# Cached attention of the decoded rows: one row on 128 partitions, or two rows on 64 each

## The chip, the cores and the metric

The kernel runs on one core of a Trainium2 chip. The core has five engines with an instruction stream each: TensorE (PE in the profile; its weight loads are PEld), VectorE (DVE), ScalarE (ACT), GpSimd (POOL) and SyncE (SP, which here only issues transfers); sixteen DMA engines move data between the device memory and the on-chip memory of 128 partitions. Each stream runs in order and waits on semaphores where it needs another engine's or a transfer's result. The metric is the device time in microseconds of one execution, the median of several runs.

## What is computed

One layer of a decoder on 256 prompt tokens and 8 decoded rows (one token each, with its own caches), D = 2048: a mixing group, cross-attention to 256 memory tokens, and a gated feed-forward part. All is float32. The change touches only the cross-attention of the 8 decoded rows, which read their memory's keys and values from caches:

```python
N_MEM, XA_HEADS, XA_DH = 256, 4, 512          # DEC_BATCH = 8

xq = (rmsnorm(x, g_xa) @ w_xa_q).reshape(B, L, XA_HEADS, XA_DH)
s = jnp.einsum('blhd,bmhd->bhlm', xq, mk) * (XA_DH ** -0.5)
p = jax.nn.softmax(s, axis=-1)
o = jnp.einsum('bhlm,bmhd->blhd', p, mv).reshape(B, L, D_MODEL)
x = x + o @ w_xa_o
```

For a decoded row `mk` and `mv` are `cache_mem_k` and `cache_mem_v` of that row: 4 heads of 256 tokens by 512 features, so 32 tiles (head, row) of 512 KB of keys and as many of values. For the prompt rows `mk` and `mv` are products of the memory with `w_k` and `w_v`, worked out in the same stretch of the kernel.

## The kernel before

**Weights.** The 264 columns (256 tokens and 8 rows) stay on chip; the weights stream past. SP loads them in halves of a step, 512 KB each, into five buffers `raw`. ScalarE copies a half to its high part, VectorE subtracts to get the low part (both into `w`, four buffers), and TensorE makes three products of the parts for each block (`mm`). The list of steps is w_in, w_out, 16 tiles of w_q, then for each of 4 heads 4 of w_k and 4 of w_v, 16 of w_o, and the feed-forward part.

**Order.** Everything beside the weights' products is written as generators that `side` starts and that are advanced between steps by a price for each `yield`; a scheduler that simulates the engines then sets the final order of instructions. Each engine executes its stream in that order. Tiles made by `B(...)` come from one rotating pool of 26 buffers. The helpers that record the engine operations all stand on line 60, so groups are told apart by their tiles.

**Cached attention.** `evac_q` writes the queries of the decoded rows, tile by tile, into `qsm` [128, 16, 8]: partition = feature within a tile of 128, then tile, then row. After the fourth tile `onesr` (128x128 ones) is made and two generators start. `dec_k` goes over heads h and rows b: GpSimd loads the keys `kcT[h, b]` and the values `vcT[h, b]`, each into a fresh tile of `B` [128, 4, 256] (partition = feature, then feature tile, then token); ScalarE makes the first product with the row's query into `dw` [128, 256], VectorE adds the three others, ScalarE copies the result to a high part `ds`, GpSimd subtracts for the low part. `dec_v` sums `ds` over the partitions with two matmuls by `onesr` (the sum is then the same in all partitions, in `ax`), takes the maximum (VectorE), the exponential and its sum (ScalarE, into `ssm`), and multiplies the four value tiles with it in place, each with its sum over tokens into one column of `osm` (VectorE). At most two (head, row) units are between the two generators (`NFL`). When the eight rows of a head are done, `osm` is multiplied by 1 / `ssm` and `st["dh"]` is raised; `attend(h)`, the prompt's attention of that head, waits for that before it folds `osm` into the input of w_o.

The same stretch holds the products of w_q's second part, w_k and w_v, the evictions of those (`B<-mm`, `t<-mm`) and GpSimd's stores of keys and values (`o_k`, `o_v`).

Of the kernel before, what the change touches and what calls it, by code (L numbers as in the profile page):

```python
# [10 lines left out]
F32 = mybir.dt.float32  # L11
F32R = mybir.dt.float32r
I32 = mybir.dt.int32
AF = mybir.ActivationFunctionType
OP = mybir.AluOpType
AX = mybir.AxisListType

P = 128
D = 2048
KC = D // P  # L20
T = 256
NS = 8
N = T + NS
RGB = 8
H = 4
# [16 lines left out]
STEP = object()  # L42
# [52 lines left out]
def layer_kernel(ctx: ExitStack, tc, xT, memT, vec, wrg, w_in, w_out, w_q, w_k, w_v, w_o,  # L95
# [3 lines left out]
    act, dve, pe = Engine(nc.scalar, price_act), Engine(nc.vector, price_dve), Engine(nc.tensor, price_pe)  # L99
    pool_e, sp = nc.gpsimd, nc.sync  # L100

    const = ctx.enter_context(tc.tile_pool(name="const", bufs=1))
# [11 lines left out]
    def nm(s):  # L114
        uid[0] += 1
        return f"{s}_{uid[0]}"

    def B(shape, dt=F32):
        return sb.tile(shape, dt, tag="B", bufs=NB, name=nm("B"))
# [15 lines left out]
    class Arr:  # L135


        def __init__(self, nb, w=N, dt=F32):
            self.t, self.nb, self.w, self.dt = {}, nb, w, dt
# [7 lines left out]
        def __call__(self, c):  # L147
            return self.tile(c // 4)[:, c % 4, :]
# [107 lines left out]
    def by2(x):  # L256

        return x.rearrange("p (a b) -> p a b", b=2)

    def turn(x):  # L260

        return x.rearrange("p (b a) -> p a b", b=2)

    def halves(x):

        return x.rearrange("p (b a) -> p b a", b=2)

    def unturn(ps):

        return ps.rearrange("p (a b) -> p b a", b=2)  # L270
# [9 lines left out]
    st = {}  # L280
# [21 lines left out]
    def side(g, prio=0):  # L302
        x = Gen(g, prio)
        gens.append(x)
        gens.sort(key=lambda q: q.prio)
        return x
# [23 lines left out]
    ones = const.tile([P, P], F32, name="ones")  # L330
    dve.memset(ones, 1.0)
    def bank(tag="mm"):
        return psm.tile([P, 512], F32, tag=tag, bufs=4, name=nm(tag))
# [10 lines left out]
    onesr = const.tile([P, P], F32R, name="onesr")  # L344
# [774 lines left out]
    qsm = const.tile([P, KC, NS], F32, name="qsm")  # L1119
    osm = const.tile([P, KC, NS], F32, name="osm")  # L1120
    ssm = const.tile([P, H, NS], F32, name="ssm")

    def evac_q(j):
        def f(ps):
            if j == 0:
                qn["t"] = Arr(KC, T)
            p2, m = unturn(ps[:, :N]), N // 2
            dve.tensor_mul(qn["t"](j)[:, :m], p2[:, 0, :], rstd[:, :m])
            dve.tensor_mul(qn["t"](j)[:, m:T], p2[:, 1, : T - m], rstd[:, m:T])
            dve.tensor_mul(qsm[:, j, :], p2[:, 1, T - m:], rstd[:, T:N])  # L1130
            qn["n"] = j + 1
            if j == 3:
                with tc.issue_after(st["split"].ins):
                    act.activation(onesr, ones, AF.Copy)
                st["dk"] = side(dec_k(), 5)
                st["dv"] = side(dec_v(), 4)
        return f

    pairs = []
    infl = {"n": 0}  # L1140

    def dec_k():
        for h in range(H):
            while qn["n"] < 4 * h + 4:
                yield STEP
            for b in range(NS):
                while infl["n"] >= NFL:
                    yield STEP
                infl["n"] += 1
                kc = B([P, 4, T])  # L1150
                pool_e.dma_start(kc, kcT[h, b])  # L1151
                w = sb.tile([P, 264], F32, tag="dw", bufs=2, name=nm("dw"))
                ws = sb.tile([P, 2, T], F32R, tag="ds", bufs=2, name=nm("ds"))
                vc = B([P, 4, T])
                pool_e.dma_start(vc, vcT[h, b])
                acc = w[:, 0:T]
                q = [qsm[:, 4 * h + c, b: b + 1] for c in range(4)]
                act.activation(acc, kc[:, 0, :], AF.Copy, scale=q[0])
                for c in range(1, 4):
                    dve.scalar_tensor_tensor(acc, kc[:, c, :], q[c], acc, op0=OP.mult, op1=OP.add)  # L1160
                act.activation(ws[:, 0], acc, AF.Copy)
                pool_e.tensor_sub(ws[:, 1], acc, ws[:, 0].bitcast(F32))  # L1162
                pairs.append((h, b, w, vc, ws))
                yield 1.1

    def dec_v():
        done, cur = 0, None
        while done < H * NS:
            nxt = None
            if pairs:  # L1170
                nxt = pairs.pop(0)
                ps = bank("ax")
                pe.matmul(by2(ps[:, :T]), onesr, turn(nxt[4][:, 0]), start=True, stop=False)
                pe.matmul(by2(ps[:, :T]), onesr, turn(nxt[4][:, 1]), start=False, stop=True)
                nxt += (ps,)
            cur, todo = nxt, cur
            if todo is None:
                yield STEP
                continue
            h, b, w, vc, _, ps = todo  # L1180
            mx, p = w[:, T: T + 1], w[:, :T]
            dve.tensor_reduce(mx, ps[:, :T], axis=AX.X, op=OP.max)
            dve.tensor_scalar(mx, mx, -XSCALE, None, op0=OP.mult)
            act.activation(halves(p), unturn(ps[:, :T]), AF.Exp, scale=XSCALE, bias=mx,
                           accum_out=ssm[:, h, b: b + 1])
            yield 0.5
            for c in range(4):
                dve.scalar_tensor_tensor(vc[:, c, :], vc[:, c, :], 1.0, p, op0=OP.mult, op1=OP.mult,
                                         accum_out=osm[:, 4 * h + c, b: b + 1])
            infl["n"] -= 1  # L1190
            done += 1
            if done % NS == 0:
                dve.reciprocal(ssm[:, h, :], ssm[:, h, :])
                for c in range(4):
                    dve.tensor_mul(osm[:, 4 * h + c, :], osm[:, 4 * h + c, :], ssm[:, h, :])
                st["dh"] = h + 1
            yield STEP

# [238 lines left out]
    for i, (src, cols, pef, evf, need) in enumerate(steps):  # L1437
# [24 lines left out]
        ps = pef(i)  # L1462
# [139 lines left out]
```

## Time and profile before

| | us |
|---|---|
| median of 3 runs (lowest, highest) | 1456.94 (1456.13, 1457.64) |
| the profiled execution | 1455.83 |
| its span | 1454.1 |
| PE busy | 1439.2 (99%) |
| DVE busy | 1045.1 (72%) |
| ACT busy | 794.9 (55%) |
| POOL busy | 128.3 (9%) |
| loads of `kcT` / `vcT`: issue to landing, median | 8.2 / 9.1 |

The span goes from the first to the last instruction of the profiled execution; the time of that execution holds what lies around it. Shares are of the span. A matmul's busy time counts its way through the array, so the time that one takes from the next is read from the timeline, start to start. Idle time of an engine counts only where another that sets the end waits for it. The first loads of `kcT` are issued at 336.7 us, the last at 600.3 us.

### The profile page before, as it was taken

The numbers are of one execution on the slowest core, as the hardware profiler recorded it, in microseconds if no ns is written. First come the engines' busy times: TensorE is split into PE (matmuls) and PEld (weight loads), VectorE is DVE, ScalarE is ACT, GpSimd is POOL, SyncE is SP. The second block draws the span as 40 slices with busy tenths as digits, with TensorE's granted clock in tenths as the row PEclk, the third lists the DMA queues.
The fourth block names the chain that finished last, engine by engine and source line by source line (L and its number), as shares of the span: only waits on it lengthen the run. The fifth ranks groups of instructions, "written<-read, shape, count | busy, mean of one in ns | idle before, by whom it ended". The sixth has DMA issues, their size and how long they took to land.

```text
span 1454.1 us, 30126 instructions
## 1 busy us (share of the span) xinstructions
PE 1439.2 (99%) x12071; PEld 1415.5 (97%) x12071; DVE 1045.1 (72%) x1999; ACT 794.9 (55%) x1279; POOL 128.3 (9%) x204
## 2 busy tenths in 40 slices
PE   9999999999999999999999999999999999999997
PEld 8999999999999999999999999999999999999997
DVE  7966797898899999987675666555665655565564
ACT  7678685666556666655544444434444443444463
POOL 0001210000124343410000000000000000000000
PEclk9999999999999999999999999999999999999999
DMA  9645896557799877955555555555555555555563
GB/s 288 234 171 179 268 363 231 177 178 271 254 344 355 340 284 297 375 172 192 197 195 194 197 193 201 190 202 190 198 194 196 196 198 194 195 197 192 172 195 112
DMA packets 99757, 326.02 MB, mean 224 GB/s; under 512 B 10944, under 2 KB 19824, under 8 KB 99616
## 3 DMA queue, kind: packets, MB, share of 16 engines
q1 hardware_dynamic: 83616, 269.84, 52.8%
q0 software_dynamic: 15136, 53.16, 10.2%
q8 instruction: 94, 1.54, 0.4%
q10 hardware_dynamic: 864, 1.09, 0.2%
q14 instruction: 47, 0.39, 0.1%
HBM read 312.78 MB, written 11.28 MB: 223 GB/s over the span
## 4 chain that ended last, share of the span: by engine, by line
PE 94%; ACT 2%; DMA 1%; DVE 1%; issue 1%; SPq 0%; POOL 0%; DVEq 0%; POOLq 0%
PE mm L60 90%; PE ax L60 5%; DMA raw<-w_in 1%; ACT B L60 1%; DVE B L60 1%; DMA B<-scr 0%; ACT w L60 0%; DVE w L60 0%; ACT L60 0%; SPq L213 0%; ACT dw L60 0%; DVE ds L60 0%; SPq L1412 0%; DMA scr<-lt 0%; ACT t L60 0%
## 5 line engine op out<-in xcount | busy, mean ns | idle before, releaser
L60 PE MATMUL mm<-B,w 128*128 128x264 f32 (+1 forms) x10960 | 1281.2, 279 | 2.5 <-DVE w L60 2.1
L60 PEld LDWEIGHTS mm<-B,w 128*128 128x128 f32 x10960 | 1260.6, 189 | 10.7 <-DVE w L60 2.4
L60 DVE TENSOR_TENSOR w<-raw,w 128x1024 fp32r<-128x1024 f32 (+1 forms) x522 | 625.4, 1200 | 312.9 <-ACT w L60 312.2
L60 ACT ACTIVATE w<-raw 128x1024 fp32r<-128x1024 f32 (+1 forms) x522 | 536.0, 1028 | 531.8 <-PE mm L60 370.8
L60 PE MATMUL mm<-w,B 128*128 128x512 f32 x384 | 86.5, 380 | 0.0
L60 PEld LDWEIGHTS mm<-w,B 128*128 128x128 f32 x384 | 70.7, 189 | 9.4
L1494 POOL TENSOR_TENSOR B<-B,rstd 128x264 f32<-128x264 f32 x4 | 2.8, 741 | 802.8 <-ACT rstd L60 802.8
L60 DVE TENSOR_TENSOR t<-mm,rstd 128x264 f32<-128x264 f32 x96 | 41.4, 432 | 28.8 <-PE mm L60 28.7
L60 DVE SCALAR_TENSOR_TENSOR B<-B,dw 128x256 f32<-128x256 f32 x128 | 52.2, 461 | 3.2 <-ACT dw L60 2.9
L60 DVE TENSOR_TENSOR xres<-xres,mm 128x264 f32<-128x264 f32 (+1 forms) x81 | 34.2, 424 | 27.2 <-PE mm L60 27.1
L60 DVE SCALAR_TENSOR_TENSOR dw<-B,qsm,dw 128x256 f32<-128x256 f32 x96 | 48.6, 512 | 0.8
L60 PE MATMUL ax<-B,B 128*128 128x256 f32 (+3 forms) x288 | 46.0, 302 | 0.8 <-DVE B L60 0.8
L1162 POOL TENSOR_TENSOR ds<-dw,ds 128x256 fp32r<-128x256 f32 x32 | 36.8, 1151 | 106.9 <-ACT ds L60 104.7
L60 PEld LDWEIGHTS ax<-B,B 128*128 128x128 f32 x288 | 39.9, 191 | 3.0 <-DVE B L60 1.0
L60 ACT ACTIVATE B<-xres,vecs 128x264 fp32r<-128x264 f32 (+1 forms) x64 | 32.1, 502 | 3.5 <-DVE xres L60 1.6
L60 ACT ACTIVATE t<-xres 128x264 f32<-128x264 f32 (+1 forms) x53 | 21.0, 409 | 16.0 <-DVE xres L60 16.0
L1151 POOL DMA_DIRECT2D B<-kcT x32 | 17.4, 544 | 122.8 <-DVE B L60 109.7
L60 DVE SCALAR_TENSOR_TENSOR B<-xres,vecs,B 128x264 fp32r<-128x264 f32 x48 | 23.3, 488 | 4.3 <-ACT B L60 4.3
L60 ACT ACTIVATE dw<-B,qsm 128x256 f32<-128x256 f32 x32 | 16.2, 507 | 16.3 <-issue 6.4
L60 ACT ACTIVATE B<-t 128x264 fp32r<-128x264 f32 (+1 forms) x60 | 24.1, 409 | 1.7 <-DVE t L60 1.5
L60 ACT ACTIVATE dw<-B,B 128x128 f32<-128x128 f32 x64 | 20.9, 390 | 7.1 <-DMA B<-scr 6.3
L60 ACT ACTIVATE dw<-ax,dw 128x256 f32<-128x256 f32 x32 | 15.0, 470 | 17.7 <-DVE dw L60 14.0
(172 smaller groups left out, 691.2 us busy)
## 6 DMA issues: line engine op xcount, KB each, us to landing
raw<-w_gu SPq DMA_DIRECT2D x176, 512.0 KB, 3.6
raw<-w_d SPq DMA_DIRECT2D x80, 512.0 KB, 3.7
raw<-w_in SPq DMA_DIRECT2D x74, 512.0 KB, 5.2
raw<-w_out SPq DMA_DIRECT2D x32, 512.0 KB, 3.8
B<-kcT POOLq DMA_DIRECT2D x32, 512.0 KB, 8.2
raw<-w_q SPq DMA_DIRECT2D x32, 512.0 KB, 5.4
B<-vcT POOLq DMA_DIRECT2D x32, 512.0 KB, 9.1
raw<-w_k SPq DMA_DIRECT2D x32, 512.0 KB, 5.1
```

The costliest lines, as they stand in the source:

```text
L60: return f(*a, **k)
L1151: pool_e.dma_start(kc, kcT[h, b])
L1162: pool_e.tensor_sub(ws[:, 1], acc, ws[:, 0].bitcast(F32))
L1494: e.tensor_mul(st["y"](c), st["y"](c), r)
```

## The change

Two rows share the partitions: a unit is now a pair of rows, one with 64 features in the lower 64 partitions and one with 64 in the upper. A pair's keys are two tiles [128, 4, 256], in which the halves are crossed in the second one, so a pair has 8 products for the scores and 8 for the values; there are 16 pairs. `onesr` is block-diagonal (two blocks of 64x64 ones), so that one sum over partitions gives both rows' scores, each in its own half.

`swap_q(h)` brings the queries into that layout (`q2`): four copies of 64x16 on GpSimd, and two small transfers that cross the halves by way of `q3`. `swap_o(h)` does the reverse with the results. They use the same two tiles, as `o2` and `o3`.

The tiles of the caches no longer come fresh from `B`: `Ring` keeps two tiles for K and two for V through the whole stage. A tile is loaded again, by two transfers of 64 partitions and 256 KB each, after the fourth product with it was issued.

```diff
@@ -1129,70 +1129,131 @@
             dve.tensor_mul(qn["t"](j)[:, m:T], p2[:, 1, : T - m], rstd[:, m:T])
             dve.tensor_mul(qsm[:, j, :], p2[:, 1, T - m:], rstd[:, T:N])
             qn["n"] = j + 1
+            if j % 4 == 3:
+                swap_q(j // 4)
             if j == 3:
                 with tc.issue_after(st["split"].ins):
-                    act.activation(onesr, ones, AF.Copy)
+                    act.activation(onesr, ones, AF.Copy, scale=0.0)
+                    for part in (LOW, HIGH):
+                        act.activation(onesr[part, part], ones[part, part], AF.Copy)
                 st["dk"] = side(dec_k(), 5)
                 st["dv"] = side(dec_v(), 4)
         return f
 
     pairs = []
     infl = {"n": 0}
+    NB2 = NS // 2
+    q2 = const.tile([P, H, 2, 4, NB2], F32, name="q2")
+    q3 = const.tile([P, H, 4, NB2], F32, name="q3")
+    o2, o3 = q2, q3
+    LOW, HIGH = slice(0, 64), slice(64, P)
+
+    def rows_of(h, even):
+        return slice(4 * h, 4 * h + 4), slice(0, NS, 2) if even else slice(1, NS, 2)
+
+    def swap_q(h):
+        for part, even in ((LOW, True), (HIGH, False)):
+            c, b = rows_of(h, even)
+            pool_e.tensor_copy(q2[part, h, 0], qsm[part, c, b])
+            c, b = rows_of(h, not even)
+            pool_e.tensor_copy(q3[part, h], qsm[part, c, b])
+        pool_e.dma_start(q2[LOW, h, 1], q3[HIGH, h])
+        pool_e.dma_start(q2[HIGH, h, 1], q3[LOW, h])
+
+    def swap_o(h):
+        rec = ssm[:, h, 0: NB2]
+        dve.reciprocal(rec, rec)
+        o = o2[:, h].rearrange("p g c b -> p (g c) b")
+        dve.tensor_mul(o, o, rec.rearrange("p (c b) -> p c b", c=1).to_broadcast([P, 8, NB2]))
+        pool_e.dma_start(o3[LOW, h], o2[HIGH, h, 1])
+        pool_e.dma_start(o3[HIGH, h], o2[LOW, h, 1])
+        for part, even in ((LOW, True), (HIGH, False)):
+            c, b = rows_of(h, even)
+            pool_e.tensor_copy(osm[part, c, b], o2[part, h, 0])
+            c, b = rows_of(h, not even)
+            pool_e.tensor_copy(osm[part, c, b], o3[part, h])
+
+    class Ring:
+        def __init__(self, src):
+            self.t, self.at = [B([P, 4, T]), B([P, 4, T])], 0
+            self.src = src
+            self.load()
+            self.load()
+
+        def load(self):
+            u = self.at
+            if u < H * NB2 * 2:
+                self.at = u + 1
+                for q, part in enumerate((LOW, HIGH)):
+                    pool_e.dma_start(self.t[u % 2][part],
+                                     self.src[u // NS, u // 2 % NB2 * 2 + q, HIGH if (u + q) % 2 else LOW])
+
+        def __call__(self, j):
+            return self.t[j // 4][:, j % 4, :]
 
     def dec_k():
+        kr = Ring(kcT)
+        st["vr"] = Ring(vcT)
+        yield STEP
         for h in range(H):
             while qn["n"] < 4 * h + 4:
                 yield STEP
-            for b in range(NS):
+            for b in range(NB2):
                 while infl["n"] >= NFL:
                     yield STEP
                 infl["n"] += 1
-                kc = B([P, 4, T])
-                pool_e.dma_start(kc, kcT[h, b])
                 w = sb.tile([P, 264], F32, tag="dw", bufs=2, name=nm("dw"))
                 ws = sb.tile([P, 2, T], F32R, tag="ds", bufs=2, name=nm("ds"))
-                vc = B([P, 4, T])
-                pool_e.dma_start(vc, vcT[h, b])
                 acc = w[:, 0:T]
-                q = [qsm[:, 4 * h + c, b: b + 1] for c in range(4)]
-                act.activation(acc, kc[:, 0, :], AF.Copy, scale=q[0])
-                for c in range(1, 4):
-                    dve.scalar_tensor_tensor(acc, kc[:, c, :], q[c], acc, op0=OP.mult, op1=OP.add)
+                for j in range(8):
+                    q = q2[:, h, j // 4, j % 4, b: b + 1]
+                    if j == 0:
+                        act.activation(acc, kr(0), AF.Copy, scale=q)
+                    else:
+                        dve.scalar_tensor_tensor(acc, kr(j), q, acc, op0=OP.mult, op1=OP.add)
+                    if j % 4 == 3:
+                        kr.load()
+                    if j == 3:
+                        yield 1.0
                 act.activation(ws[:, 0], acc, AF.Copy)
                 pool_e.tensor_sub(ws[:, 1], acc, ws[:, 0].bitcast(F32))
-                pairs.append((h, b, w, vc, ws))
+                pairs.append((h, b, w, ws))
                 yield 1.1
 
     def dec_v():
         done, cur = 0, None
-        while done < H * NS:
+        while done < H * NB2:
             nxt = None
             if pairs:
                 nxt = pairs.pop(0)
                 ps = bank("ax")
-                pe.matmul(by2(ps[:, :T]), onesr, turn(nxt[4][:, 0]), start=True, stop=False)
-                pe.matmul(by2(ps[:, :T]), onesr, turn(nxt[4][:, 1]), start=False, stop=True)
+                pe.matmul(by2(ps[:, :T]), onesr, turn(nxt[3][:, 0]), start=True, stop=False)
+                pe.matmul(by2(ps[:, :T]), onesr, turn(nxt[3][:, 1]), start=False, stop=True)
                 nxt += (ps,)
             cur, todo = nxt, cur
             if todo is None:
                 yield STEP
                 continue
-            h, b, w, vc, _, ps = todo
+            h, b, w, _, ps = todo
             mx, p = w[:, T: T + 1], w[:, :T]
             dve.tensor_reduce(mx, ps[:, :T], axis=AX.X, op=OP.max)
             dve.tensor_scalar(mx, mx, -XSCALE, None, op0=OP.mult)
             act.activation(halves(p), unturn(ps[:, :T]), AF.Exp, scale=XSCALE, bias=mx,
                            accum_out=ssm[:, h, b: b + 1])
             yield 0.5
-            for c in range(4):
-                dve.scalar_tensor_tensor(vc[:, c, :], vc[:, c, :], 1.0, p, op0=OP.mult, op1=OP.mult,
-                                         accum_out=osm[:, 4 * h + c, b: b + 1])
+            for j in range(8):
+                v = st["vr"](j)
+                dve.scalar_tensor_tensor(v, v, 1.0, p, op0=OP.mult, op1=OP.mult,
+                                         accum_out=o2[:, h, j // 4, j % 4, b: b + 1])
+                if j % 4 == 3:
+                    st["vr"].load()
+                if j == 3:
+                    yield 1.0
             infl["n"] -= 1
             done += 1
-            if done % NS == 0:
-                dve.reciprocal(ssm[:, h, :], ssm[:, h, :])
-                for c in range(4):
-                    dve.tensor_mul(osm[:, 4 * h + c, :], osm[:, 4 * h + c, :], ssm[:, h, :])
+            if done % NB2 == 0:
+                swap_o(h)
+                yield STEP
                 st["dh"] = h + 1
             yield STEP
 
```

What the change does to the streams of VectorE and GpSimd is shown at two places in the middle of the second part of w_q, where the cached attention of the first head runs. The names carry the number of the buffer and of its use; a new pair of numbers is a new tile.

VectorE in the kernel before: `dw` are score products of one row (`dw_680` reads the keys `B_679`), `B_671,osm` are value products, `w<-raw` weight splits, `B_672` evictions of w_q's tiles.

```order
L60 TENSOR_TENSOR w_693_5738<-raw_676_5625,w_693_5738 128x8x128
L60 SCALAR_TENSOR_TENSOR dw_680_5641<-B_679_5639,qsm_112,dw_680_5641 128x256
L60 TENSOR_REDUCE dw_669_5556<-ax_678_5629 128x1
L60 TENSOR_TENSOR B_672_5566<-mm_685_5660,rstd_94 128x132
L60 TENSOR_TENSOR B_672_5566<-mm_685_5660,rstd_94 128x124
L60 TENSOR_TENSOR qsm_112<-mm_685_5660,rstd_94 128x8
L60 TENSOR_SCALAR dw_669_5556<-dw_669_5556 128x1
L60 TENSOR_TENSOR w_694_5741<-raw_677_5627,w_694_5741 128x8x128
L60 SCALAR_TENSOR_TENSOR B_671_5558,osm_113<-B_671_5558,dw_669_5556 128x256 x4
L60 TENSOR_TENSOR w_703_5822<-raw_686_5709,w_703_5822 128x8x128
L60 TENSOR_REDUCE dw_680_5641<-ax_688_5713 128x1
L60 SCALAR_TENSOR_TENSOR dw_690_5725<-B_689_5723,qsm_112,dw_690_5725 128x256
```

Each row's keys and values have a tile of their own: the score product in the last row reads keys that no row above has used.

VectorE in the changed kernel around the same eviction of w_q: `B_628_5235` is the second K tile of the ring, `B_627_5234` the first, `dw_653` and `dw_666` two pairs that follow one another.

```order
L60 SCALAR_TENSOR_TENSOR dw_653_5486<-B_628_5235,q2_115,dw_653_5486 128x256
L60 SCALAR_TENSOR_TENSOR dw_666_5648<-B_627_5234,q2_115,dw_666_5648 128x256
L60 TENSOR_TENSOR w_674_5732<-raw_664_5636,w_674_5732 128x8x128
L60 SCALAR_TENSOR_TENSOR dw_653_5486<-B_628_5235,q2_115,dw_653_5486 128x256
L60 SCALAR_TENSOR_TENSOR dw_666_5648<-B_627_5234,q2_115,dw_666_5648 128x256
L60 TENSOR_TENSOR B_660_5577<-mm_670_5665,rstd_94 128x132
L60 TENSOR_TENSOR B_660_5577<-mm_670_5665,rstd_94 128x124
L60 TENSOR_TENSOR qsm_112<-mm_670_5665,rstd_94 128x8
L60 SCALAR_TENSOR_TENSOR dw_666_5648<-B_627_5234,q2_115,dw_666_5648 128x256
L60 TENSOR_TENSOR w_675_5735<-raw_665_5638,w_675_5735 128x8x128
L60 TENSOR_TENSOR w_682_5826<-raw_671_5714,w_682_5826 128x8x128
L60 SCALAR_TENSOR_TENSOR dw_666_5648<-B_628_5235,q2_115,dw_666_5648 128x256 x2
```

The fourth row is the last product of pair `dw_653` with `B_628_5235`; the last row is the next pair's first with the same tile, after it was loaded again. Seven rows lie between them.

GpSimd in the kernel before, at that place: loads of keys (L1151) and values (L1155), and the low parts of the scores (L1162).

```order
L1162 TENSOR_TENSOR ds_681_5642<-dw_680_5641,ds_681_5642 128x256
L1155 DMA B_712_5895<-vcT 128x1024
L1162 TENSOR_TENSOR ds_691_5726<-dw_690_5725,ds_691_5726 128x256
L1151 DMA B_720_5981<-kcT 128x1024
L1155 DMA B_723_5985<-vcT 128x1024
L1162 TENSOR_TENSOR ds_701_5810<-dw_700_5809,ds_701_5810 128x256
L1151 DMA B_730_6065<-kcT 128x1024
L1155 DMA B_733_6069<-vcT 128x1024
L1151 DMA B_740_6149<-kcT 128x1024
L1155 DMA B_743_6153<-vcT 128x1024
L1162 TENSOR_TENSOR ds_711_5894<-dw_710_5893,ds_711_5894 128x256
L1151 DMA B_750_6217<-kcT 128x1024
```

The loads stand in front of subtractions that belong to rows loaded earlier: `ds_711` comes after the keys and values of three later rows.

GpSimd in the changed kernel at that place: refills of the ring (L1188, two transfers each; `B_629_5240` and `B_630_5241` are the two V tiles), the low parts (L1219), the queries' copies (L1157, L1159) and their transfers across the halves (L1160, L1161).

```order
L1188 DMA B_627_5234<-kcT 64x1024 x2
L1188 DMA B_629_5240<-vcT 64x1024 x2
L1188 DMA B_630_5241<-vcT 64x1024 x2
L1188 DMA B_628_5235<-kcT 64x1024 x2
L1219 TENSOR_TENSOR ds_654_5487<-dw_653_5486,ds_654_5487 128x256
L1188 DMA B_627_5234<-kcT 64x1024 x2
L1157 COPY q2_115<-qsm_112 64x16
L1159 COPY q3_116<-qsm_112 64x16
L1157 COPY q2_115<-qsm_112 64x16
L1159 COPY q3_116<-qsm_112 64x16
L1161 DMA q2_115<-q3_116 64x16
L1160 DMA q2_115<-q3_116 64x16
```

Each load now waits for the fourth product with the same tile. Behind the second K tile's refill stands the low part of that pair's scores. On TensorE the only difference is that 64 matmuls `ax<-ds,onesr` have become 32; SP's stream is the same row for row.

## The prediction

> **What bounds the kernel now.** I read the page first: busy time, then the chain that ended last.
>
> ```profile
> span 1454.1 us, 30126 instructions
> PE 1439.2 (99%) x12071; PEld 1415.5 (97%) x12071; DVE 1045.1 (72%) x1999; ACT 794.9 (55%) x1279; POOL 128.3 (9%) x204
> PE 94%; ACT 2%; DMA 1%; DVE 1%; issue 1%; SPq 0%; POOL 0%; DVEq 0%; POOLq 0%
> L60 PE MATMUL mm<-B,w 128*128 128x264 f32 (+1 forms) x10960 | 1281.2, 279 | 2.5 <-DVE w L60 2.1
> ```
>
> TensorE is busy 99% of the span and its largest group waited 2.5 us in all. So a matmul that goes is worth its time, and work on other engines is worth nothing unless it makes TensorE wait. The order of both programs is the same before the decoded rows' attention and again from the third output tile of w_o on, so only that stretch can move. Its stretches of 40 us follow; behind the interval stand its length, then busy us and instructions of PE, PEld, DVE, ACT and POOL, granted clock, DMA share and GB/s.
>
> ```profile
> 360.00:400.00 40.00, 40.00 (x356) 39.94 (x356) 32.44 (x70) 20.35 (x26) 6.58 (x9) 1.00 0.73 267
> 400.00:440.00 40.00, 40.00 (x358) 40.00 (x357) 38.39 (x111) 22.23 (x37) 10.35 (x16) 1.00 0.90 339
> 440.00:480.00 40.00, 40.00 (x248) 36.81 (x247) 39.62 (x97) 25.76 (x44) 19.40 (x28) 1.00 0.98 372
> 480.00:520.00 40.00, 40.00 (x235) 36.44 (x234) 38.74 (x99) 26.32 (x50) 16.76 (x19) 1.00 0.84 308
> 520.00:560.00 40.00, 40.00 (x240) 36.58 (x239) 39.03 (x100) 25.07 (x51) 14.16 (x20) 1.00 0.88 332
> 560.00:600.00 40.00, 40.00 (x236) 36.45 (x235) 38.25 (x99) 25.85 (x52) 16.84 (x24) 1.00 0.78 290
> 600.00:640.00 40.00, 40.00 (x244) 36.67 (x243) 38.80 (x103) 27.30 (x58) 11.46 (x15) 1.00 0.72 267
> ```
>
> TensorE never rests here, but it rests nowhere on slack either: from 400 to 640 us VectorE, which splits every weight tile for TensorE, is idle only 1.61 + 0.38 + 1.26 + 0.97 + 1.75 + 1.20 = 7.2 us of 240, and the DMA engines are at 0.72 to 0.98. A wait that VectorE takes on here has almost no room.
>
> **The matmuls that go.** Sixteen pairs instead of 32 rows, two sums each: 64 become 32.
>
> ```profile
> L60 PE MATMUL ax<-ds,onesr 128*128 128x256 f32 x64 | 17.1, 277 | 0.0
> 444.18 0.27 PE L60 MATMUL ax<-ds,onesr 128*128 128x256 f32 x1
> 444.29 0.95 PE L60 MATMUL mm<-B,w 128*128 128x264 f32 x7
> ```
>
> The mean of 277 ns is the latency in the pipeline; in the timeline (start, length) the next matmul starts 0.11 us after one. So 32 × 0.11 = **3.5 us** leave TensorE. This is the sure part.
>
> **VectorE's work.** The score chains go from 32 × 3 to 16 × 7 multiply-adds (+16), the value products stay 128; 16 maxima, 16 scalings and the 16 products of 128x8 by 1/sum go, four of 128x32 come.
>
> ```profile
> L60 DVE SCALAR_TENSOR_TENSOR dw<-B,qsm,dw 128x256 f32<-128x256 f32 x96 | 48.6, 512 | 0.8
> L60 DVE SCALAR_TENSOR_TENSOR B<-B,dw 128x256 f32<-128x256 f32 x128 | 52.2, 461 | 3.2 <-ACT dw L60 2.9
> L60 DVE TENSOR_REDUCE dw<-ax 128x1 f32<-128x256 f32 x32 | 13.3, 416 | 0.3 <-PE ax L60 0.2
> L60 DVE TENSOR_SCALAR dw<-dw 128x1 f32<-128x1 f32 x32 | 4.7, 147 | 0.2
> L60 DVE TENSOR_TENSOR osm<-osm,ssm 128x8 f32<-128x8 f32 x16 | 1.6, 158 | 0.0
> ```
>
> +16 × 0.512 = +8.2; −16 × (0.416 + 0.147) = −9.0; −1.6 for the products; four of 128x32, no row of their own, between 0.158 and 0.461 each: about +0.8. Net −1.6 us. ScalarE loses 48 activations of about half a microsecond and GpSimd 16 subtractions of 1.15 us; both have room in every stretch above, so this is worth nothing. GpSimd gains 32 copies of 64x16 (no row; between the 0.16 us of a 128x8 operation on VectorE and the 1.15 us of the 128x256 subtraction), 80 DMA issues at 0.54 us net: 43 us more issuing and 5 to 37 us of copies, less 18 us of subtractions. It has some 150 of 240 us free, so this too I cost at nothing by itself.
>
> **The query exchange.** The first head's first scores now wait for four copies and a small transfer: in the new order about 4.2 us of VectorE's work lie between the fourth query tile and the first product with exchanged queries, while two issues (1.1 us) and the shortest landing seen for a cache tile (3.8 us, quoted below) take 4.9 and a median one 9.5. That is 1 to 6 us late, once, at some 375 us, where VectorE is idle 7.6 us of 40: covered. The other three heads' queries are ready a pair or more ahead. The exchange of results has 17 us of VectorE's order between the last product and the fold that uses it: covered.
>
> **The ring.** This is the term that decides. Before, each K and V tile is a fresh buffer of the large pool, and loads are issued in bursts well ahead of their use. In the change K has two tiles and V two, and a tile is loaded again only after its fourth use. All that covers a refill then is VectorE's order between that use and the first use of the refill. I priced the rows of the new order by start-to-start times:
>
> ```profile
> 446.25 0.47 DVE L60 SCALAR_TENSOR_TENSOR dw<-B,qsm,dw 128x256 f32<-128x256 f32 x1
> 446.65 1.21 DVE L60 TENSOR_TENSOR w<-raw,w 128x1024 fp32r<-128x1024 f32 x1
> 447.79 0.99 DVE L60 SCALAR_TENSOR_TENSOR dw<-B,qsm,dw 128x256 f32<-128x256 f32 x2
> 448.69 0.48 DVE L60 TENSOR_TENSOR B<-mm,rstd 128x132 f32<-128x132 f32 x2
> 449.09 0.16 DVE L60 TENSOR_TENSOR qsm<-mm,rstd 128x8 f32<-128x8 f32 x1
> 598.53 0.43 DVE L60 SCALAR_TENSOR_TENSOR B<-B,dw 128x256 f32<-128x256 f32 x1
> 598.88 0.42 DVE L60 SCALAR_TENSOR_TENSOR B<-B,dw 128x256 f32<-128x256 f32 x1
> ```
>
> Score product 0.42, weight split 1.16, two evictions 0.40, queries 0.10, value product 0.35. The place shown with the change: after the last use of `B_628_5235` come two score products (0.84), the three evictions (0.5) and two weight splits (2.32), 3.7 us, and then the refilled tile is read. Of 60 refills the shortest covers are 3.7, 4.1, 4.3, 5.5, 5.7, 6.3, 6.5, 6.8, 7.5, 7.6, 7.9, 8.0, 8.0, 8.3, 8.3, 8.5; the rest are 9 to 19 us. Most of the short ones are K tiles, the second above all.
>
> How long a refill takes, from the trace of before (issues from 360 to 660 us, KB each, median us to landing; then the shortest, median and longest of the whole run, K's line first):
>
> ```profile
> B<-kcT POOLq DMA_DIRECT2D x30, 512.0 KB, 8.4
> B<-vcT POOLq DMA_DIRECT2D x30, 512.0 KB, 9.5
> L1151 POOL DMA_DIRECT2D B<-kcT x32 | 17.4, 544 | 122.8 <-DVE B L60 109.7
> DMA to landing us min/median/max: 3.8/8.2/13.9
> DMA to landing us min/median/max: 4.3/9.1/15.9
> ```
>
> A refill is two issues, one after the other, so 0.54 us more: 4.3 us at best, 8.9 at K's median, 10.0 at V's, 14.4 at K's longest. The medians come out of bursts, in which a tile stands behind others, which speaks for less; the new tile stands behind the refills of the three other tiles, the weight loads and GpSimd's own queue, which speaks for as much. I take 8.9, the median of K, as the late ones are K's. Each refill then lacks 8.9 less its cover: 35 us over the sixteen; since a stall inside the cover of another refill lengthens that cover, running down the order with the stalls added leaves **29 us in 12 stalls** (largest 5.2). The same sum gives 1.4 us at 4.5, 6.5 at 6, 12 at 7, 20 at 8, 42 at 10.
>
> What a stall delays is the weight split behind it, and so TensorE. It is paid back out of VectorE's idle 7.2 us and the 1.6 us of work that went: 8.8. Left: 29 − 8.8 = 20 us.
>
> Sum: 1454.1 − 3.5 + 20 = 1470.8 us of span. The median of the runs shown, 1456.94, lies 2.8 above the span (the profiled execution itself took 1455.83): **1473.6 us**.
>
> [...]
>
> **The rivals.**
>
> *Refills come in time.* A tile that finds the queue empty lands in 3.8 us, and the new loads come one by one instead of in bursts. With 4.3 to 6 us the stalls are 1 to 6.5 us, less than the 8.8 that VectorE can give: only the matmuls count, 1454.1 − 3.5 + 2.8 = 1453.4. For it: the bursts make the medians. Against: from 440 to 480 us DMA stands at 0.98. Faster, chance 0.26.
>
> *It cancels.* Refills of about 7.5 us, 16 us of stalls, 7 left over, 3.5 gained: 1460; at 7 us 1456.6. Chance 0.13 that it ends within 0.2%.
>
> *Half-width loads cost double.* A refill writes 64 partitions at a time; if the DMA engines take as long for a half as for a whole tile, the stretch becomes DMA's. At 440 to 480 us they moved 372 / 0.98 = 380 GB/s, so 512 KB hold all sixteen for 1.38 us, and 60 refills would cost 83 us more. Free in 360 to 640 us are 40 × (0.27 + 0.10 + 0.02 + 0.16 + 0.12 + 0.22 + 0.28) = 47 us. Left 36: 1454.1 − 3.5 + 36 + 2.8 = 1489. It decides as soon as a half-width tile holds the engines over 47 / 60 = 0.8 us longer. [...] Chance 0.21.
>
> *The sum is not halved.* Two features' sums share a product only if the ones tile is block-diagonal; the two 64x64 activations make it so, and the count of matmuls in the order is 32. No chance of its own.
>
> **How the numbers follow.** Forecast, some refills late by several microseconds: 0.40, with its own range 1460 (7.5 us) to 1486 (10 us: 42 − 8.8 − 3.5 = +30). Two measurements differ by about 0.2%, 2.9 us, without a cause, so faster is below 1454.0, slower above 1459.9. Faster 0.26, same 0.13, slower 0.40 + 0.21 = 0.61. The range reaches from just under the rival of refills in time, 1452, to the double price, 1490; outside remain a chain of longer landings and a gain beyond the matmuls.
>
> **What would show it.** 32 `ax<-ds,onesr` in place of 64: the first term. VectorE's score products and ScalarE's first product of a pair waiting for DMA `B<-kcT`, on the second K tile first: the ring. TensorE's `mm<-B,w` waiting on VectorE's `w` between 400 and 620 us by about 20 us. Landings of `B<-kcT` at 8 to 9 us: my price; at 4 to 6: the first rival; a DMA share near 1.0 at fewer GB/s than 372, with longer landings of `raw` too: half-width loads. If TensorE shows 99% and no DMA wait stands on VectorE, my ring term is wrong as a whole.

## The result, and the profile after

| | before | changed |
|---|---|---|
| median of 4 runs, us | 1456.67 | 1511.72 |
| lowest, highest | 1456.13, 1457.64 | 1507.25, 1516.58 |
| profiled execution, its span | 1455.83, 1454.1 | 1507.25, 1505.5 |

The changed kernel is slower by 55 us: ratio 1.0375, 95% interval 1.0358 to 1.0392. The prediction, 1473.6 with a range up to 1490, had the direction and not the size.

The page of the changed kernel, busy time and two groups:

```profile
PE 1457.5 (97%) x12039; PEld 1426.0 (95%) x12039; DVE 1043.0 (69%) x1971; ACT 773.2 (51%) x1217; POOL 162.0 (11%) x300
L60 PE MATMUL mm<-B,w 128*128 128x264 f32 (+1 forms) x10960 | 1293.5, 280 | 12.6 <-DVE w L60 9.8
L60 PE MATMUL ax<-ds,onesr 128*128 128x256 f32 x32 | 10.7, 341 | 17.0 <-ACT ds L60 16.6
```

32 matmuls are gone, and yet TensorE is busy for 18 us longer and idle for 48 us instead of 15. The section on the change calls the 32 the only difference on TensorE; that is so for the number of matmuls and not for their order, in which 338 of the other 12,007 stand at another place. Where the time goes, the stretches of 40 us show (columns as in the prediction: PE, PEld, DVE, ACT, POOL, granted clock, DMA share, GB/s):

```profile
360.00:400.00 40.00, 40.00 (x356) 39.94 (x356) 32.30 (x65) 17.42 (x23) 6.53 (x13) 1.00 0.85 255
400.00:440.00 40.00, 35.04 (x286) 34.34 (x285) 30.29 (x94) 16.85 (x24) 18.27 (x32) 0.94 0.95 258
440.00:480.00 40.00, 35.14 (x232) 33.18 (x231) 31.03 (x81) 16.39 (x24) 20.84 (x38) 0.89 1.01 266
480.00:520.00 40.00, 37.08 (x192) 32.66 (x191) 33.09 (x75) 17.91 (x30) 14.67 (x25) 0.96 1.03 283
520.00:560.00 40.00, 36.43 (x197) 32.06 (x196) 33.92 (x85) 20.86 (x42) 21.14 (x36) 0.96 1.03 294
560.00:600.00 40.00, 34.53 (x195) 30.77 (x193) 33.01 (x92) 18.30 (x36) 14.96 (x28) 0.96 1.02 276
600.00:640.00 40.00, 34.86 (x177) 29.70 (x177) 33.84 (x78) 18.53 (x36) 16.23 (x32) 0.96 1.03 281
640.00:680.00 40.00, 37.23 (x208) 32.99 (x207) 33.02 (x81) 21.62 (x42) 14.40 (x22) 0.96 0.77 246
```

From 440 to 640 us the DMA engines are busy all the time and move 266 to 294 GB/s; before they moved 372 in their fullest stretch, 440 to 480 us, at a share of 0.98. VectorE, which had no room before, now stands 6 to 10 us of every 40. TensorE stands too, 2.8 to 5.5 us of every 40 from 400 to 680 us, and its clock is granted at 0.89 to 0.96.

The transfers by queue from 440 to 640 us (packets, MB, share of the 16 engines' time), of the kernel before and of the changed one; q0 carries GpSimd's transfers, the caches above all, q1 SP's, the weights:

```profile
q1 hardware_dynamic: 9854, 35.89, 48.4%
q0 software_dynamic: 7565, 26.67, 35.1%
```

```profile
q0 software_dynamic: 8501, 26.75, 51.9%
q1 hardware_dynamic: 7969, 29.04, 50.0%
```

MB over the share of 200 us gives the rate while a queue is served. GpSimd's goes from 26.67 / 70.2 = 380 GB/s to 26.75 / 103.8 = 258, and the weights', whose transfers are the same as before, from 371 to 290. The waits for caches, for the score sums and for weight tiles in the changed kernel from 360 to 720 us follow (us in all, times, longest); GpSimd's waits and ScalarE's others are left out:

```profile
ACT dw L60 <- DMA B<-kcT: 36.2, 7, 8.5
DVE dw L60 <- DMA B<-kcT: 29.2, 8, 6.7
PEld ax L60 <- ACT ds L60: 19.4, 9, 5.1
PE ax L60 <- ACT ds L60: 16.6, 8, 4.9
PEld mm L60 <- DVE w L60: 10.6, 6, 4.0
DVE B L60 <- DMA B<-vcT: 9.6, 6, 2.7
PE mm L60 <- DVE w L60: 7.9, 5, 3.7
```

One such chain in the timeline (start, length; in brackets the idle time before and what ended it): a K refill issued at 411.31, ScalarE waiting 6.31 us for it, VectorE behind it, the high part `ds` behind VectorE, and TensorE standing at the score sum.

```profile
411.31 1.03 POOL L1188 DMA_DIRECT2D B<-kcT  x2 [1.98 <-issue]
420.87 0.51 ACT L60 ACTIVATE dw<-B,q 128x256 f32<-128x256 f32 x1 [6.31 <-DMA B<-kcT]
424.01 0.42 ACT L60 ACTIVATE ds<-dw 128x256 fp32r<-128x256 f32 x1 [0.74 <-DVE dw L60]
424.48 0.38 PE L60 MATMUL ax<-ds,onesr 128*128 128x256 f32 x1 [2.07 <-ACT ds L60]
```

Three causes were open: the transfers into 64 partitions, the rings of two tiles, and the doubled number of transfers.

### The profile page after: what moved, and what is told of

Same layout as the page of the kernel before. It is cut to its first block, busy times and chain, and to the rows that moved or that the text cites. A ratio compares the mean times of both kernels' runs of the same rounds, so it can differ in the third digit from the quotient of the medians.

```text
span 1505.5 us, 30081 instructions
## 1 busy us (share of the span) xinstructions
PE 1457.5 (97%) x12039; PEld 1426.0 (95%) x12039; DVE 1043.0 (69%) x1971; ACT 773.2 (51%) x1217; POOL 162.0 (11%) x300
## 4 chain that ended last, share of the span: by engine, by line
PE 55%; DMA 1%; DVE 1%; issue 0%; ACT 0%; DVEq 0%; POOL 0%; ACTq 0%
PE mm L60 54%; DVE B L60 1%; DMA B<-vcT 1%; PE ax L60 1%; DMA B<-kcT 1%; DVE dw L60 0%; DVE w L60 0%; DVE c L60 0%; DVE t L60 0%; DVEq L1640 0%; POOL B L1188 0%; ACT t L60 0%; DVE xres L60 0%; ACT w L60 0%; ACT c L60 0%
## 5 line engine op out<-in xcount | busy, mean ns | idle before, releaser
L60 DVE SCALAR_TENSOR_TENSOR dw<-B,q,dw 128x256 f32<-128x256 f32 x112 | 57.6, 518 | 35.3 <-DMA B<-kcT 29.2
L1188 POOL DMA_DIRECT2D B<-kcT x64 | 33.2, 523 | 189.9 <-DVE B L60 101.8
L1188 POOL DMA_DIRECT2D B<-vcT x64 | 33.1, 522 | 38.8 <-DVE B L60 33.8
L60 ACT ACTIVATE dw<-B,q 128x256 f32<-128x256 f32 x16 | 8.1, 508 | 51.8 <-DMA B<-kcT 36.2
L60 PE MATMUL ax<-ds,onesr 128*128 128x256 f32 x32 | 10.7, 341 | 17.0 <-ACT ds L60 16.6
L60 PEld LDWEIGHTS ax<-ds,onesr 128*128 128x128 f32 x32 | 6.5, 206 | 20.8 <-ACT ds L60 19.4
## 6 DMA issues: line engine op xcount, KB each, us to landing
raw<-w_k SPq DMA_DIRECT2D x32, 512.0 KB, 10.3
```

Source lines behind the costliest of these rows:

```text
L60: return f(*a, **k)
L1188: pool_e.dma_start(self.t[u % 2][part], self.src[u // NS, u // 2 % NB2 * 2 + q, HIGH if (u + q) % 2 else LOW])
```

## The experiments

All medians are beside runs of the kernel before on the same chip (1455.9 to 1457.0 us). In the kernels with even and odd partitions or whole transfers from the changed kernel the caches are laid out in pairs before the launch, as the other inputs are laid out; the data that reach a tile are the same. An edit can also move the scheduler's order; where the order on every engine stays the same, the text says so.

**1. The same transfers, other partitions.**

```diff
-                for q, part in enumerate((LOW, HIGH)):
-                    pool_e.dma_start(self.t[u % 2][part],
-                                     self.src[u // NS, u // 2 % NB2 * 2 + q, HIGH if (u + q) % 2 else LOW])
+                for part in (slice(0, P, 2), slice(1, P, 2)):
+                    pool_e.dma_start(self.t[u % 2][part], self.src[u // NS, u % NS, part])
```

> The changed kernel with one thing altered: the two transfers of a refill write the even and the odd partitions instead of the lower and the upper 64 (the caches are laid out in pairs beforehand, the data in the tiles are the same). Same number of transfers, same bytes, same order on every engine. Theory 'lower and upper half cost double': the DMA share of 440 to 640 us falls from 1.02 to about 0.85 at over 300 GB/s, landings of raw w_k fall from 10.3 to 5 or 6 us, and 1453 to 1475 us remain, what the ring of two tiles costs. Theory 'ring of two tiles': 1505 to 1515, as the change. Theory 'twice as many transfers of half the size': 1505 to 1515 too.

Measured 1473.76 us, ratio 1.0112 (1.0096 to 1.0129). This one edit takes 38 of the 55 us away, with every instruction in its place. The rows that a transfer reads in device memory step by two along with the partitions. Whole transfers read neighbouring rows and are served at 380 GB/s before, so neighbouring rows are not what makes the halves slow. Queues from 440 to 640 us:

```profile
q1 hardware_dynamic: 9324, 33.94, 47.4%
q0 software_dynamic: 9184, 28.88, 42.4%
```

GpSimd's queue is served at 28.88 / 84.8 = 341 GB/s, the weights at 33.94 / 94.8 = 358. From 400 to 640 us the DMA share is 0.81 to 0.96, and `raw<-w_k` lands after 6.9 us instead of 10.3 (expected were 5 or 6).

**2. Deeper rings, still lower and upper halves.** Three tiles each for K and V; a third load at the start, and the tile of a product chosen by a count of uses.

```diff
-            self.t, self.at = [B([P, 4, T]), B([P, 4, T])], 0
+            self.t, self.at, self.use = [B([P, 4, T]) for _ in range(3)], 0, 0
```

> The changed kernel with three K tiles and three V tiles in the rings, still loaded by lower and upper 64 partitions. Theory 'lower and upper half cost double': the DMA engines stay at 1.0 in the stage, 1485 to 1512 us. Theory 'ring of two tiles': waits for the kcT and vcT transfers on VectorE and ScalarE (39 and 36 us in the change) go below 10, 1453 to 1470.

Measured 1503.76, ratio 1.0328 (1.0297 to 1.036): 8 us better than the change. The waits for `kcT` fell as the ring's theory said, from 65 us to 11, but those for `vcT` rose from 9.6 to 19.0 and the time stayed where the other theory put it:

```profile
ACT w L60 <- DMA raw<-w_k: 27.5, 14, 2.7
DVE B L60 <- DMA B<-vcT: 19.0, 6, 5.1
ACT w L60 <- DMA raw<-w_q: 17.2, 9, 3.6
DVE dw L60 <- DMA B<-kcT: 9.4, 3, 3.9
ACT dw L60 <- DMA B<-kcT: 1.7, 1, 1.7
```

With caches ordered earlier, the weights come late in their place; from 400 to 640 us the DMA share is 1.03 throughout.

**3. and 4. The kernel before, with its loads cut in two.** Only this differs between them, and their order is the same row for row:

```diff
-                pool_e.dma_start(kc, kcT[h, b])
+                for part in (slice(0, 64), slice(64, P)):        # 3; in 4: (slice(0, P, 2), slice(1, P, 2))
+                    pool_e.dma_start(kc[part], kcT[h, b, part])
```

and the same for `vc`.

> The kernel before with each load of a cache tile made by two transfers, lower and upper 64 partitions; fresh tiles from the large pool as before. Theory 'lower and upper half cost double': 1485 to 1510 us, DMA share near 1.0 at about 280 GB/s from 440 us on. Theory 'ring of two tiles': there is no ring here, 1456 to 1462. Theory 'twice as many transfers': 1470 to 1510.

> The kernel before with each load of a cache tile made by two transfers, even and odd partitions; the order is that of the kernel with lower and upper halves, row for row. Theory 'lower and upper half cost double': 1455 to 1462 us. Theory 'ring of two tiles': 1456 to 1462. Theory 'twice as many transfers': the same as with lower and upper halves, 1470 to 1510.

Measured 1511.74 (ratio 1.0377, 1.0346 to 1.0407) and 1470.91 (1.01, 1.0085 to 1.0115). Without ring and pairs, loads cut into halves cost as much as the whole change. Even and odd partitions cost 41 us less, but 14 more than whole transfers, which I had not expected of them. The rates from 440 to 640 us, worked out as above, are 263 GB/s for GpSimd's queue and 289 for the weights with halves, and 375 and 358 with even and odd partitions. With even and odd partitions TensorE stood at the end of the stage, for the last scores (stretches of 20 us; PE, PEld, DVE, ACT, POOL, clock, DMA share, GB/s):

```profile
620.00:640.00 20.00, 18.28 (x113) 16.41 (x111) 19.54 (x47) 12.39 (x25) 7.10 (x10) 1.00 0.80 288
640.00:660.00 20.00, 14.09 (x97) 13.60 (x98) 16.99 (x64) 10.09 (x28) 2.97 (x4) 0.74 0.22 76
```

GpSimd had waited 17.6 us in this stage for earlier cache transfers of its own before it issued further ones, and cutting the loads also let the scheduler choose another order. Which of the two made the scores late was not separated.

**5. Even and odd, three tiles.**

> Even and odd partitions, and three tiles each for K and V. If what even and odd partitions left (1473.8 us with two tiles) is the ring's, the waits for kcT on VectorE and ScalarE (13 and 15 us there) go to a few us and 1452 to 1460 remain. If it is the price of twice as many transfers, 1468 to 1476 remain.

Measured 1461.27, ratio 1.003 (1.0019 to 1.0041). The waits for `kcT` are 2.2 us on VectorE, where they were 13.2 in 1, and ScalarE has none of its 15.2 left; 12.5 of the 17 us that remained in 1 are gone, which ends just above the first band. So that part goes with the third tile; the order changed with it, and how much of the 12.5 us is the order's was not separated. The order on every engine is that of 2, which takes 42.5 us longer: a third pair of kernels in which only the partitions differ.

**6. and 7. Whole transfers, two and three tiles.** One transfer of 128 partitions per refill, `pool_e.dma_start(self.t[u % 2], self.src[u // NS, u % NS])`; in 7 with `% 3`.

> The changed kernel with one transfer of 128 partitions and 512 KB per refill (caches laid out in pairs beforehand), two tiles each for K and V. If what even and odd partitions left is the ring's, about the same: 1465 to 1475 us, with waits for kcT. If it is the number of transfers: 1452 to 1460.

> One transfer of 128 partitions per refill and three tiles each for K and V: both costs taken out. Either theory: 1452 to 1458 us; 1453.4 if only the 32 matmuls count.

Measured 1491.26 (1.0236, 1.0222 to 1.025) and 1461.74 (1.0034, 1.0022 to 1.0047). Both were expected lower. In 6 the scheduler chose another order, and its covers are shorter: by the prediction's prices 2.7, 3.2, 3.7, 3.7, 3.7, 3.9, 4.1 us are the shortest, where the change has 3.7, 4.1, 4.3, 5.5. At 6 us a refill the prediction's running sum gives 19 us of stalls for this order, 6.5 for that of the change; K tiles land after 6.1 us here. Over the 1453.4 us of the arithmetic alone they cost 38 and 20 us: the ranking of the two orders is right, and both cost well over their stalls. 5 and 7 lie 0.5 us apart with 128 and 64 cache transfers, so in a ring of three the doubled number of transfers shows no cost, although the order of the two differs.

**8. No ring, whole transfers.** The pairs' arithmetic with tiles fresh from the pool, four loads at the head of a pair.

> The pairs' arithmetic of the change, but loaded as before: no ring, every tile fresh from the large pool, one transfer of 128 partitions each. If the ring's short covers are all that three tiles each left over 1453.4 us (1461 to 1462 measured there), 1452 to 1456, a gain of the 32 matmuls. If pairs cost TensorE something of their own (it waits for the scores' sums, or the exchange of queries and results), 1458 to 1465.

Measured 1462.33, ratio 1.0038 (1.0026 to 1.0051): with whole transfers and no ring the pairs are still no gain. The timeline shows one place:

```profile
533.43 1.20 POOL L1202 TENSOR_TENSOR ds<-dw,ds 128x256 fp32r<-128x256 f32 x1 [10.47 <-ACT ds L60]
534.58 1.08 POOL L1188 DMA_DIRECT2D B<-kcT  x2
541.16 0.51 ACT L60 ACTIVATE dw<-B,q 128x256 f32<-128x256 f32 x1 [6.05 <-DMA B<-kcT]
```

GpSimd stood 10.5 us at a subtraction, with the next pair's loads behind it.

**9. Half the dose.** Keys by even and odd partitions, values by halves, the order that of 1.

> The changed kernel with the keys refilled by even and odd partitions and only the values by lower and upper 64; same order on every engine as with even and odd for both (1473.8 us) and as the change (1511.7). If half-width transfers add their time from the first byte, half of the 38 us: 1490 to 1496. If they cost only once the DMA engines are full, the free time takes most of it: 1474 to 1484, with a DMA share of 0.93 to 1.0.

Measured 1485.94, ratio 1.0197 (1.0181 to 1.0212): between the two bands. The values' half costs 12 us and the keys' half the other 26; neither a price per byte nor a threshold alone says that. The values' refills have covers of 7.5 us and more, the keys' from 3.7, which would make a longer landing cost less for values, but this was not tried by itself.

**10. Loads one pair ahead.** As 8, with the four loads of the next pair written before the products of this one.

> As with fresh tiles and whole transfers (1462.3 us), but the four loads of a pair are written one pair ahead. There, from 523 to 533 us GpSimd stood at a subtraction of ds while the next pair's four loads waited behind it, and ScalarE then waited 6.0 us for kcT. If such blocked loads are what is left, no wait for kcT over 2 us remains and 1453 to 1457 us are reached. If the pairs cost TensorE something else, 1460 to 1464 stay.

Measured 1467.62, ratio 1.0082 (1.0068 to 1.0096), worse than 8, though the waits for `kcT` are 0.8 us in all. Of the 9.8 us that TensorE stands from 400 to 640 us, 8.0 lie at one place: 16 value products in a row on VectorE (427.25 to 432.87 us) ahead of w_q's evictions, and TensorE waits until the last of those, `qsm`, is done.

```profile
433.54 12.71 PE L60 MATMUL mm<-B,w 128*128 128x264 f32 x96 [8.01 <-DVE qsm L60]
```

**11. and 12. Smaller lumps.** 10, and 7, with the generators giving way after four products:

```diff
                     if j == 3:
-                        yield 1.0
+                        yield STEP
...
                 if j == 3:
                     yield 1.0
+                    yield STEP
```

> Loads one pair ahead, and the generators give way after four products instead of eight, so that 3.8 us is the longest stretch of attention work on VectorE without a weight split or an eviction (5.8 with the loads ahead alone, where TensorE stood 8.0 us at one place behind 16 value products in a row). If such lumps are what is left with loads in time, 1453 to 1457 us; if the pairs cost TensorE something else, 1460 or more.

> The ring of three with whole transfers (1461.7 us), with the generators giving way after four products. Longest stretch of attention work 3.6 us. If lumps are what is left there, 1453 to 1458; if it is the ring's covers (5.2 us the shortest, with landings of 5 to 6 us), 1459 to 1463.

Both 1453.59 us: ratios 0.9978 (0.9969 to 0.9986) and 0.9979 (0.997 to 0.9988), 3.4 us faster than the kernel before. The stretches of 11 from 400 to 560 us:

```profile
400.00:440.00 40.00, 40.00 (x358) 40.00 (x357) 39.24 (x116) 20.25 (x28) 11.94 (x24) 1.00 0.90 311
440.00:480.00 40.00, 40.00 (x249) 36.87 (x249) 38.04 (x92) 21.99 (x33) 20.69 (x37) 1.00 1.00 387
480.00:520.00 40.00, 40.00 (x239) 36.50 (x238) 39.02 (x95) 24.39 (x48) 18.15 (x26) 1.00 0.83 292
520.00:560.00 40.00, 39.88 (x238) 36.24 (x238) 37.39 (x86) 24.14 (x45) 10.70 (x17) 1.00 0.83 298
```

TensorE stands for 0.1 us and the clock is whole. 12 is the change itself with whole transfers, a third tile in each ring and smaller lumps.

12 is 8 us faster than 7, of which 6 are less standing from 400 to 640 us (239.81 us busy against 233.85), and that standing was not behind a lump of products on VectorE. TensorE's waits from 360 to 700 us, the largest of 7 and then the only one of 12:

```profile
PE ax L60 <- POOL ds L1218: 5.4, 6, 1.8
```

```profile
PE ax L60 <- DVE B L60: 0.2, 1, 0.2
```

In 7 TensorE stands at score sums, for the low part `ds` that GpSimd subtracts. The three longest of these waits (1.85, 1.48 and 1.22 us) each follow copies of the exchange of queries or results, which stand in front of the subtraction in GpSimd's stream; twice the copies had themselves waited, 5.81 and 3.34 us, for the exchange's small transfers. One of the three:

```profile
448.35 1.66 POOL L1174 COPY osm<-q 64x16 f32<-64x16 f32 x2 [5.81 <-DMA q<-q]
451.10 1.44 POOL L1218 TENSOR_TENSOR ds<-dw,ds 128x256 fp32r<-128x256 f32 x1
452.59 0.38 PE L60 MATMUL ax<-ds,onesr 128*128 128x256 f32 x1 [1.22 <-POOL ds L1218]
```

At this place of 12 the subtraction stands ahead of those copies (450.83 against 454.35 us).

## Why the prediction was wrong

**The matmuls that go: right.** 32 instead of 64, 3.5 us predicted; with nothing else in the way the pairs give 1456.95 − 1453.59 = 3.4 us.

**The half-width transfers: chosen wrongly, and priced in the wrong place.** This is the step that failed. The forecast's sum took the landing of a whole tile for a refill and put the extra time of a half-width refill on the DMA engines at nothing. "Half-width loads cost double" stood beside it as a rival with a chance of 0.21. Its factor of two was the author's assumption, as no row of before shows a cache load of 64 partitions; that such loads hold the DMA engines longer is what happened: they were served at 258 GB/s instead of 380. Experiments 1, 3 against 4, and 2 against 5 show it with the order on every engine unchanged: 38, 41 and 42.5 us. The signs that the prediction named for it came, a DMA share of 1.0 at fewer GB/s and `raw<-w_k` landing after 10.3 us. So did the sign named for its own price: K tiles land after 8.0 us in the changed kernel, because they are half-width, and after 5.8 in experiment 1.

The rival's price was off in its parts: at 258 instead of 380 GB/s a cache tile holds the engines 1.47 times as long, not twice, which is 60 tiles × 1.38 us × 0.47 = 39 us instead of 83; but the weights, at 290 instead of 371 GB/s, were not priced at all. The 101 halves of weights that VectorE splits from 360 to 660 us in the kernel before hold them 0.52 MB / 290 − 0.52 MB / 371 = 0.4 us longer each, some 40 us. The sum, 79, comes near the 83 by luck. Less the 47 us of free DMA time it leaves 32, an estimate, beside the 38 to 42.5 measured.

**The cases were set against each other and add.** The forecast held the ring for the cost and the half-width loads for a rival. Both came: 1454.1 − 3.5 + 20 (ring) + 36 (what the free DMA time does not take of 83) + 2.8 = 1509.4, by the prediction's own terms, beside 1511.7. That it comes so near is luck, as the working of both terms is off. That the costs add is shown: halves cost 38 us with two tiles, 42.5 with three and 41 without a ring, so neither cost used up the other's slack.

**The ring: the size right for a wrong reason.** Without the half-width cost (experiment 1) the change gives 1473.76, the forecast 1473.6. But the price of a landing, 8.9 us, was too long: there the transfers land after 5.8 us (K) and 5.3 (V), so a refill takes about 6.3, and the prediction's own running sum gives some 8 us of stalls there, not 29. The step "it is paid back out of VectorE's idle" failed the other way. A late K tile delays the scores `ds`, and TensorE, which runs in order, stands at the sum over them, 4.1 us in experiment 1 and 16.6 in the changed kernel; time that VectorE has free elsewhere does not bring that back. Of the 20 us, 12.5 went with a third tile (5) and nearly 8 more are gone in 12.

**A term that was put at nothing: GpSimd's stream.** The prediction gave GpSimd's copies and transfers no cost, as it has 150 of 240 us free, and called the exchange covered. Free time in all does not help a subtraction that stands behind copies in the same stream: in 7 TensorE stands 5.4 us for it, 4.6 of them behind the exchange's copies, and 7 is 8 us slower than 12. In the changed kernel itself this is small, 0.3 us of TensorE's waits. In 11 and 12 the exchange costs nothing that a trace shows.

**A term that was missing: lumps.** The sum had VectorE's work as a total only. 16 value products in a row, 5.6 us, made TensorE stand 8.0 us in 10; 11, with smaller lumps, is 14 us faster, though the order of other instructions moves with that edit too. That lumps cost the changed kernel something is not shown: by the prediction's prices its longest stretch of attention work on VectorE without a weight split or an eviction is 3.8 us, where before has 2.9, but 11 has 3.8 and 12 has 3.6 as well, and both lose nothing.

**The other terms.** The order on SP is unchanged and hid nothing.

## What to carry to other kernels

Which partitions a transfer writes counted here as its bytes did: transfers into the lower and the upper half were served at 258 GB/s instead of 380 and slowed even the full-width transfers of another queue, from 371 to 290, so lay data out beforehand and load 128 partitions at once. Where a stage has as little slack as this one, costs of different kinds can add (halves cost 38, 42.5 and 41 us with a ring of two, of three and none); don't let one stand as the alternative of the other. And before halving the number of units, look at what each in-order engine has in front of the instruction that the bottleneck waits for, and not at its free time in all: 16 products on VectorE in 10 (8.0 us of standing), copies on GpSimd in 7 (4.6 us).

## What was not expected of the hardware

**In 10 standing cost TensorE more than the time it stood.** Stretches of 5 us of experiment 10, around the 8 us (same columns):

```profile
420.00:425.00 5.00, 4.04 (x34) 3.66 (x32) 4.81 (x8) 2.73 (x4) 2.67 (x4) 1.00 1.02 398
425.00:430.00 5.00, 0.38 (x1) 0.19 (x1) 4.43 (x19) 1.02 (x4) 0.10 (x1) 0.67 1.02 408
430.00:435.00 5.00, 1.46 (x7) 1.49 (x8) 5.00 (x32) 0.63 (x2) 1.75 (x4) 0.50 0.79 250
435.00:440.00 5.00, 5.00 (x37) 5.00 (x37) 5.00 (x14) 1.74 (x3) 4.86 (x12) 0.80 0.43 158
440.00:445.00 5.00, 5.00 (x47) 5.00 (x46) 3.62 (x5) 2.55 (x4) 4.02 (x7) 1.00 0.87 313
```

While TensorE stands here the granted clock falls to 0.67 and then to 0.50, and work begins again slowly: 7 instructions in the 1.46 us from 433.54 (0.21 us each), 37 in the next 5 us and 47 in the 5 us after (0.11 us each). Taken as 0.50 first and 1 after, the 0.80 from 435 to 440 us is 2 us at 0.50, which puts the return of the whole clock, as an estimate, at 437.0, 3.5 us after the work began.

10 is 14.0 us slower than 11; 9.7 us of it is more standing from 400 to 640 us (230.18 us busy against 239.88). In the changed kernel the clock is below 1 in every stretch from 400 to 680 us. 40 × (0.06 + 0.11 + 5 × 0.04) = 15 us is the most that this costs, an estimate, since in 10 the clock is low (0.50 to 0.67) while TensorE stands too; the standing in these stretches is about 30 us. Together they would be most of the 51 us between the spans.

**Partitions in steps of two are not half-width.** Two transfers of 64 partitions each, even and odd, are served much like one of 128 (GpSimd's queue from 440 to 640 us): in the rings at 341 and 348 GB/s (1 and 5) beside 343, 348 and 352 (6, 7 and 12), without a ring at 375 (4) beside 380 before. The same bytes into 64 neighbours went at 258 and 263 (the change and 3).
